# A hybrid diffusion step on one core: the second feed-forward's opening, its sums on VectorE, and matmuls ahead of the last norm

## The chip, the cores and the metric

The kernel runs on one core of a Trainium2 chip. The core has a matrix engine (TensorE, PE in the profile, with its weight loads as PEld), a vector engine (VectorE, DVE), a scalar engine (ScalarE, ACT), a general-purpose engine (GpSimd, POOL), and DMA queues, of which SyncE (SP) issues most transfers. The metric is the time of one execution on the device, in microseconds; smaller is better. Three runs of the kernel before took 2042.53, 2045.99 and 2050.24 us.

## The reference, cut to what matters

The reference is one inference step of a network of two layers over 128 context tokens and 512 latent tokens with 1024 features. Layer 0 mixes tokens with neighbourhood attention and a two-way recurrent mixer, layer 1 with differential attention. Each layer ends with a gated feed-forward of 22 x 128 = 2816 hidden features; a norm over the features closes the whole.

```python
def rmsnorm(x, g):
    xf = x.astype(jnp.float32)
    r = lax.rsqrt(jnp.mean(xf * xf, -1, keepdims=True) + NORM_EPS)
    return (xf * r).astype(x.dtype) * g

def modulate(h, shift, scale):
    return h * (1.0 + scale) + shift

def swiglu(h, w1, w3, w2):
    return (jax.nn.silu(h @ w1) * (h @ w3)) @ w2
...
    for l in range(DEPTH):
...
        xs = xs + ms[2] * ys
        xs = xs + ms[5] * swiglu(modulate(rmsnorm(xs, norm_ffn[l]), ms[3], ms[4]), ffn_w1[l], ffn_w3[l], ffn_w2[l])
```

The change concerns the feed-forward of the second layer (l = 1) and the norm behind it, for all 640 tokens (context and latent, xp and xs).

## The kernel before, in words

**Layout.** Features lie on the 128 partitions in 8 tiles (KT), tokens along the free dimension. The 640 tokens are two halves of HT = 320; one matmul has 128 x 128 weights and 320 tokens. For accuracy each factor is split in a rounded part h and a rest l (`split`: ScalarE casts to h, VectorE subtracts h to get l), and each product of two tiles is three matmuls, wh·bh, wh·bl and wl·bh (`product`: four tiles along the features, so 12 matmuls).

**The second feed-forward (`bffn`, from line 627).** Its upward projections, w1 and w3, are done by a scheme after Winograd and Strassen. Two weight tiles (a_ and a_ + 11) by two halves of the features form a 2 x 2 block matrix, and features by token halves form another; seven products do instead of eight. The activations come as B["11"], "21", "22" and the combinations t1 to t4, made by `BNorm` (`apply`: lines 580 to 611, `rest`: from 612). The weights come as "11", "12", "22" and the combinations s1 to s4, made in `prep_up`: two weight tiles r1 and r2 are loaded by SyncE (L711, L712), s1 = r2[lo] + r2[hi] (L717) and s3 = r1[lo] - r2[lo] in the place of r2[lo] (L719) are made on GpSimd, s2 and s4 on VectorE (L723, L724), and four calls of `split` (L646, L647) cast them. The raw tiles have two buffers, so the load of r2 waits until the split of an earlier tile has read its buffer. `run_up` issues the seven products for one pair and one matrix in the order 11, s1, s2, 12, s3, s4, 22. Three of these write the same PSUM tile `al` one on top of the other, and ScalarE copies `al` out in between (L757 after 11, L763 after s2, L769 after s3): the following product into `al` waits for the copy. Partials lie in the tiles `top` and `bot`, taken in turn from a pool of four (`tmp`), for w1 as for w3. `close` (L659, L660) splits the gated result.

**The opening.** The first pair (a_ = 0) is not done by the seven products but by eight plain ones for each token half, in `up_first`: four weight tiles FIRST = w1[0], w1[11], w3[0], w3[11], loaded by `plain`. The first three are loaded and split ahead of layer 1's output projection (`w_out_tail`), the fourth within the opening. Eight products on the first token half (upper features "11", lower features "21") run while the norm of the second half is computed: after the first product come the norm's sums over the features, after four more the matmul that spreads the reciprocal root over the partitions, and after three more `bn.apply(1, ps)` makes the second half's activations. After each of the upper products ScalarE copies the partial to `q` (L687). Then come four products with t1, and four with 22.

**What sets the order.** A planner orders each engine's work by the order in the program and by modelled times at which operands are there; an instruction that is ready early may be put ahead of program order, but then each engine works its list strictly in turn. While `pinned[0]` is set, TensorE's matmuls keep the program's order; that holds for the opening up to its last products. Preparations are interleaved with the products: `prep(i + 1)` advances one step after each product of item i.

**Downward projection and end.** Pairs are taken in groups (0,1), (2,3), (4,5), (6,7), (8,9,10); the downward products of a group (`run_down`) follow the first pair of the next one. The last group's are done for all but three output tiles first, then for the last three by token halves, with the final norm of a half (`Last.done`) behind each. For the second half the norm is by columns: `token_sums` (twelve entries in the profile, one column each), `rsqrt_cols` (eleven small VectorE operations) and `spread_half` (three matmuls that spread the root over the partitions), then eight VectorE multiplications and eight stores.

Of the kernel before, what the change touches and what calls it, by code (L numbers as in the profile page):

```python
# [14 lines left out]
ALU = mybir.AluOpType  # L15
# [14 lines left out]
LAST = 3  # L30
URGENT = 3000
WARM = (8, 3)
NWQ = 3
GROUPS = ((0, 1), (2, 3), (4, 5), (6, 7), (8, 9, 10))
NSQ = 1
# [55 lines left out]
def tile_backbone(ctx: ExitStack, tc: tile.TileContext, I, O, stop=99):  # L91
# [174 lines left out]

    def token_sums(ps, t, first, last):
        for j, (a, b) in enumerate(WIN):
            PE.matmul(ps[:, j:j + 1], lhsT=t[:, a:b], rhs=ones32[:, 0:1], start=first and j == 0, stop=last,
                      skip_group_check=True)  # L270

    def rsqrt_cols(ps, n, scale, eps):
        m, s, t = [SM.tile([P, n], F32, tag="r" + x, name=nm("r"), bufs=1) for x in "xyz"]
# [126 lines left out]
    class Norm:  # L400
# [18 lines left out]
        def rms(self, h, cols=False):  # L419
            assert self.n[h] == KT  # L420
            acc = self.acc[h]
            pss = one()
            if cols:
                for i, t in enumerate(acc):
                    token_sums(pss, t, i == 0, i == len(acc) - 1)
                s = rsqrt_cols(pss, 3, 1.0 / D, NORM_EPS)
                pr = one()
                spread_half(pr, s)
                return pr[:, 0:HT]
            for i, t in enumerate(acc):  # L430
                for j in range(4):
                    PE.matmul(pss[32 * j:32 * j + 32, 0:80], lhsT=ones32, rhs=t[:, 80 * j:80 * j + 80],
                              start=i == 0, stop=i == len(acc) - 1, skip_group_check=True)
            r4 = rsqrt4(pss[:, 0:80], NORM_EPS, 1.0 / D)
            pr = one()
            PE.matmul(pr[:, 0:HT], lhsT=e0, rhs=r4, start=True, stop=True)
            return pr[:, 0:HT]
# [106 lines left out]
    class BNorm(Norm):  # L544
# [8 lines left out]
        def halves(self, name, src, engines):  # L553
            a, b = unit([P, 4, HT], F32R, "bh"), unit([P, 4, HT], F32R, "bl")
            self.B[name] = a, b
            for j in range(2):
                c = slice(2 * j, 2 * j + 2)
                A.copy(a[:, c], src[:, c])
                engines[j].tensor_tensor(b[:, c], src[:, c], a[:, c], ALU.subtract)

        def done(self, h):
            if h == 0:
# [46 lines left out]
        def rest(self):  # L609
            f = self.f  # L610
            t2 = self.full("t2")

            def both(fn):
                for j in range(2):
                    fn(slice(2 * j, 2 * j + 2))

            both(lambda q: V.tensor_tensor(t2[:, q], f["22"][:, q], f["11"][:, q], ALU.subtract))
            self.halves("t2", t2, (V, G))
            yield
            both(lambda q: V.tensor_tensor(f["12"][:, q], f["22"][:, q], f["12"][:, q], ALU.subtract))  # L620
            self.halves("t3", f["12"], (V, G))
            yield
            both(lambda q: V.tensor_tensor(f["21"][:, q], f["21"][:, q], t2[:, q], ALU.subtract))
            self.halves("t4", f["21"], (V, G))
            yield

    def bffn(l, bn, xs, nx, X, w2):
# [14 lines left out]
        def flat(x):  # L642
            return x.rearrange("p k c -> p (k c)")

        def split(h, l_, src):
            A.copy(h, src)  # L646
            V.tensor_tensor(l_, src, h, ALU.subtract)  # L647

        def product(ps, w, b, first):
            (wh, wl), (bh, bl) = w, b  # L650
# [21 lines left out]
        yield  # L672

        with tc.tile_pool(name=f"wq{l}", bufs=NWQ, reuse_waits="tile") as WQ, \
                tc.tile_pool(name=f"sq{l}", bufs=NSQ, reuse_waits="tile") as SQ:
            ring[1] = WQ
            G_ = {}

# [1 line left out]
            def up_first():  # L680
                q = X.tile([P, 4, HT], F32, tag="g", name=nm("q"))
                s0 = cur["p"].tile([P, 2, 512], F32, tag="s", name=nm("be"))
                first = [one("a")[:, 0:HT], one("a")[:, 0:HT], s0[:, 0, 0:HT], s0[:, 1, 0:HT]]
                for n, b in ((0, "11"), (1, "11"), (2, "11"), (0, "21"), (1, "21"), (3, "11"), (2, "21"), (3, "21")):
                    product(first[n], Ws[n][b == "21"], B[b], b == "11")
                    if b == "11":
                        A.copy(q[:, n], first[n])  # L687
# [21 lines left out]
            def prep_up(name, a_, W):  # L709
# [4 lines left out]
                h0, l0 = two()  # L714
                split(h0, l0, r1)
                s1 = SQ.tile([P, 4, P], F32, tag="s1", name=nm("s1"))
                G.tensor_tensor(s1, r2[:, lo], r2[:, hi], ALU.add)  # L717
                yield
                G.tensor_tensor(r2[:, lo], r1[:, lo], r2[:, lo], ALU.subtract)  # L719
                hs, ls = [SQ.tile([P, 4, P], F32R, tag="s" + x, name=nm("s" + x)) for x in "hl"]  # L720
                split(hs, ls, s1)
                s24 = SQ.tile([P, KT, P], F32, tag="s2", name=nm("s2"))
# [25 lines left out]
            def run_up(name, a_, W):  # L748
# [2 lines left out]
                c = pr[a_]  # L751
                beta = c["be"][:, int(name == "w3"), 0:HT]
                al, de = one("a")[:, 0:HT], one("t")[:, 0:HT]
                top = tmp([P, 2, HT], name="top")
                bot = tmp([P, 2, HT], name="bot")
                product(al, W["11"], B["11"], True)
                A.copy(top[:, 0], al)  # L757
# [31 lines left out]
            def run_down(ms, pairs, hs, last, W):  # L789
                gs = [x for p_ in pairs for x in G_[p_]]  # L790
                gh, gl = [g for g, _ in gs], [g for _, g in gs]
                for m in ms:
                    resid(xs[m], proj([W[m]], gh, gl, psum(turn()), hs), gate, m, hs, nx if last else None)
                    yield
                if last and ms[-1] == KT - 1 and hs != (0, 1):
                    nx.done(hs[0])

# [36 lines left out]
                return iter(())  # L834

            pinned[0] = True
            uf = up_first()
            next(uf)
            ps = bn.rms1(lambda: [next(uf) for _ in range(4)])
            Ws.append(plain(*FIRST[3]))  # L840
            for _ in range(3):
                next(uf)
            bn.apply(1, ps)
            rest, nxt = bn.rest(), prep(0)
            for i, _ in enumerate(uf):
                if i == 4:
# [1259 lines left out]
```

## Time and profile before

| what | us |
|---|---|
| median of 3 runs (lowest to highest) | 2045.99 (2042.53 to 2050.24) |
| the profiled execution | 2047.56 |
| its span in the trace | 2045.8 |
| TensorE busy | 1933.3 (95%) |
| VectorE busy | 1353.2 (66%) |
| ScalarE busy | 800.1 (39%) |
| GpSimd busy | 443.8 (22%) |
| the second feed-forward in the trace | from about 1575 to the end |

The mean granted clock of TensorE in the profiled execution is 0.977 of full speed. In the views a row names the line of the code, the engine, the operation and its operands (out<-in), and where an engine stood still before an instruction, that time and what ended it stand in brackets. Line 99 is the helper through which all matmuls go. Matmuls overlap, so the distance from start to start tells the rate, not the length of one. The tile names in the rows leave out numbers: `be` is a PSUM pair, `ps` and `pp` other PSUM tiles, `s` the sums of weights, `wr` a raw weight tile, `xn`, `hb`, `bh` and `bl` stages of the norm's output.

### The profile page before, as it was taken

The page shows a single profiled execution, that of the slowest core. Times are in us where ns is not written, and L with a number is a line of the kernel's source. Part 1 is how long each engine was busy: PE and PEld are TensorE (multiplying, and loading weights), DVE is VectorE, ACT ScalarE, POOL GpSimd, SP SyncE. Part 2 cuts the span into 40 slices and gives each one's busy share as a digit, 9 for nine tenths or more (in the row PEclk, how much of TensorE's full clock was granted, in tenths as well). Part 3 has the DMA queues.
Part 4 walks back from the last instruction along what each step waited for, and adds up shares of the span by engine and source line. Part 5 has one row for each costly group of instructions (what it writes and reads, how often), then busy time and mean ns, then how long its engine had stood idle before and what let it go on. Part 6 is the DMA issues. An engine that isn't in the chain of part 4 may idle for free.

```text
span 2045.8 us, 36390 instructions
## 1 busy us (share of the span) xinstructions
PE 1933.3 (95%) x14572; PEld 1720.3 (84%) x14572; DVE 1353.2 (66%) x2695; ACT 800.1 (39%) x1585; POOL 443.8 (22%) x451
## 2 busy tenths in 40 slices
PE   6888999978999999999999999999998899999998
PEld 2777787845466899999999988989988899999997
DVE  6559657656667697733772386788787866666665
ACT  3434342322445332212222255556554544343341
POOL 1233443433130210000000034233312311111100
PEclk8999999987999999999999999999999999999998
DMA  7433233262725255432442232111012132232222
GB/s 262 146 94 104 72 100 108 82 195 87 231 68 180 97 186 175 167 112 83 157 152 68 85 105 69 51 39 58 29 42 72 56 99 73 73 93 73 83 83 75
DMA packets 106129, 214.21 MB, mean 105 GB/s; under 512 B 33384, under 2 KB 43624, under 8 KB 102632
## 3 DMA queue, kind: packets, MB, share of 16 engines
q1 hardware_dynamic: 99080, 172.31, 27.1%
q0 software_dynamic: 6880, 39.59, 5.4%
q8 instruction: 114, 1.87, 0.4%
q14 instruction: 55, 0.45, 0.1%
HBM read 190.36 MB, written 23.44 MB: 105 GB/s over the span
## 4 chain that ended last, share of the span: by engine, by line
PE 63%; DVE 11%; DMA 4%; ACT 3%; issue 2%; POOL 1%; SPq 0%; ACTq 0%; DVEq 0%; POOLq 0%
PE ps L99 33%; PE pp L99 16%; PE c L99 2%; PE be L99 2%; PE sd L99 2%; DMA wr<-in_w 2%; PE psc L99 1%; PE y L99 1%; PE pj L99 1%; PE sna L99 1%; PE pa L99 1%; DVE mt L1186 1%; DVE wl L647 1%; PE po L99 1%; DVE mi L1187 1%
## 5 line engine op out<-in xcount | busy, mean ns | idle before, releaser
L344 ACT CAST wh<-wr 128x1024 fp32r<-128x1024 f32 (+3 forms) x174 | 143.1, 824 | 426.4 <-issue 189.0
L347 DVE TENSOR_TENSOR wl<-wr,wh 128x1024 fp32r<-128x1024 f32 (+2 forms) x124 | 130.4, 1054 | 130.5 <-ACT wh L344 129.6
L99 PE MATMUL ps<-hh,wh 128*128 128x320 f32 x592 | 185.7, 314 | 0.0
L99 PE MATMUL ps<-hl,wh 128*128 128x320 f32 x592 | 185.4, 313 | 0.2
L99 PE MATMUL ps<-hh,wl 128*128 128x320 f32 x592 | 185.2, 313 | 0.0
L99 PE MATMUL pj<-hh,wh 128*128 128x320 f32 x416 | 135.9, 328 | 7.6 <-ACT wh L344 5.0
L99 PE MATMUL ps<-bh,wh 128*128 128x320 f32 x432 | 134.9, 312 | 7.8 <-ACT top L757 6.4
L99 PE MATMUL pj<-hl,wh 128*128 128x320 f32 x416 | 137.5, 331 | 0.3 <-POOL hl L308 0.2
L99 PE MATMUL pj<-hh,wl 128*128 128x320 f32 x416 | 135.8, 327 | 1.5 <-POOL wl L347 1.5
L99 PE MATMUL ps<-bh,wl 128*128 128x320 f32 x432 | 134.1, 310 | 0.0
L99 PE MATMUL ps<-bl,wh 128*128 128x320 f32 x432 | 134.0, 310 | 0.0
L216 DVE SCALAR_TENSOR_TENSOR av<-wa,cs,av 128x512 f32<-128x512 f32 x182 | 123.9, 746 | 0.0
L347 POOL TENSOR_TENSOR wl<-wr,wh 128x512 fp32r<-128x512 f32 (+1 forms) x50 | 72.2, 1448 | 204.9 <-ACT wh L344 187.7
L99 PE MATMUL pp<-hh,wh 128*128 128x320 f32 x368 | 115.5, 314 | 0.0
L99 PE MATMUL pp<-hh,wl 128*128 128x320 f32 x368 | 114.0, 310 | 0.0
L99 PE MATMUL pp<-hl,wh 128*128 128x320 f32 x368 | 113.8, 310 | 0.0
L99 PEld LDWEIGHTS ps<-hh,wh 128*128 128x128 f32 x592 | 111.6, 189 | 2.2 <-ACT hh L465 0.8
L99 PEld LDWEIGHTS ps<-hl,wh 128*128 128x128 f32 x592 | 111.6, 188 | 2.1 <-issue 0.8
L99 PEld LDWEIGHTS ps<-hh,wl 128*128 128x128 f32 x592 | 111.6, 189 | 1.7 <-issue 1.5
L646 ACT CAST wh<-wr 128x1024 fp32r<-128x1024 f32 (+1 forms) x71 | 72.0, 1014 | 101.8 <-PE ps L99 61.0
L647 DVE TENSOR_TENSOR wl<-wr,wh 128x1024 fp32r<-128x1024 f32 (+1 forms) x71 | 88.8, 1251 | 16.0 <-ACT wh L646 15.8
L383 DVE SCALAR_TENSOR_TENSOR x<-ps,ada,x 128x192 f32<-128x192 f32 (+2 forms) x156 | 63.5, 433 | 50.2 <-PE ps L99 50.0
(409 smaller groups left out, 5625.9 us busy)
## 6 DMA issues: line engine op xcount, KB each, us to landing
wr<-in_w SPq DMA_DIRECT2D x88, 512.0 KB, 3.6
wa<-in_w_ada POOLq DMA_DIRECT2D x26, 1024.0 KB, 5.2
wa<-in_w_ada SPq DMA_DIRECT2D x88, 256.0 KB, 5.0
wr<-in_w_qk SPq DMA_DIRECT2D x16, 512.0 KB, 3.5
wr<-in_w2s SPq DMA_DIRECT2D x16, 512.0 KB, 3.6
wr<-in_w SPq DMA_DIRECT2D x19, 384.0 KB, 3.2
wr<-in_w_in_u SPq DMA_DIRECT2D x28, 256.0 KB, 2.9
wr<-in_w_in_qk SPq DMA_DIRECT2D x24, 256.0 KB, 2.9
```

Of the source, the lines that this page charges most:

```text
L99: i = nc.tensor.matmul(*a, **k)
L216: V.scalar_tensor_tensor(out=acc[s], in0=w[:, j], scalar=c, in1=acc[s], op0=ALU.mult, op1=ALU.add)
L344: A.copy(wh[:, 0:n], raw[:, 0:n])
L347: eng.tensor_tensor(wl[:, 0:n], raw[:, 0:n], wh[:, 0:n], ALU.subtract)
L383: V.scalar_tensor_tensor(out=xk[:, a:b], in0=pp[h][:, a - HT * h:b - HT * h], scalar=gate[:, m, s:s + 1], in1=xk[:, a:b], op0=ALU.mult, op ...
L646: A.copy(h, src)
L647: V.tensor_tensor(l_, src, h, ALU.subtract)
L1186: V.tensor_tensor(t3, bc(mi[:, rows, jj], 2, w), bc(mi[:, jj, cols], 1, jj), ALU.mult)
L1187: V.tensor_tensor(mi[:, rows, cols], mi[:, rows, cols], t3, ALU.add)
```

## The change

1. In `up_first` the four upper products ("11") come first, then the four lower ones ("21"). The fourth weight tile is loaded and split ahead of the opening, not within it.
2. The first `split` behind the opening's norm is ordered, on ScalarE and on VectorE, behind the last cast and the last subtraction of the norm (`gate_`, `lastA`, `lastV`). These are orders within an engine, without a semaphore.
3. The subtractions for the second half of t2, t3 and t4, and the weight sums s1 and s3, move from GpSimd to VectorE.
4. `top` of w3 gets a pool with one buffer of its own (`TP_`, 2,560 bytes a partition).
5. Between the column sums of the last norm and its spread, twelve matmuls on a constant operand (`cur["full"]`, the first gated tile of the last group) write the PSUM tile that the spread then overwrites; they are ordered behind the sums.

```diff
+NWARM = 12
...
     def token_sums(ps, t, first, last):
         for j, (a, b) in enumerate(WIN):
-            PE.matmul(ps[:, j:j + 1], lhsT=t[:, a:b], rhs=ones32[:, 0:1], start=first and j == 0, stop=last,
-                      skip_group_check=True)
+            i = PE.matmul(ps[:, j:j + 1], lhsT=t[:, a:b], rhs=ones32[:, 0:1], start=first and j == 0, stop=last,
+                          skip_group_check=True)
+        return i
...
-                    token_sums(pss, t, i == 0, i == len(acc) - 1)
+                    at_ = token_sums(pss, t, i == 0, i == len(acc) - 1)
                 s = rsqrt_cols(pss, 3, 1.0 / D, NORM_EPS)
                 pr = one()
+                w = cur["full"]
+                for _ in range(NWARM):
+                    i = PE.matmul(pr[:, 0:HT], lhsT=w[:, 0:P], rhs=w[:, 0:HT], start=True, stop=True)
+                    tc.add_manual_dep(i.ins, at_.ins.name, NOSYNC, reason="in between")
+                    at_ = i
                 spread_half(pr, s)
...
-                A.copy(a[:, c], src[:, c])
-                engines[j].tensor_tensor(b[:, c], src[:, c], a[:, c], ALU.subtract)
+                self.lastA = A.copy(a[:, c], src[:, c])
+                self.lastV = engines[j].tensor_tensor(b[:, c], src[:, c], a[:, c], ALU.subtract)
...
-            self.halves("t2", t2, (V, G))
+            self.halves("t2", t2, (V, V))
...
-            self.halves("t3", f["12"], (V, G))
+            self.halves("t3", f["12"], (V, V))
...
-            self.halves("t4", f["21"], (V, G))
+            self.halves("t4", f["21"], (V, V))
...
+        gate_ = [None]
+
         def split(h, l_, src):
-            A.copy(h, src)
-            V.tensor_tensor(l_, src, h, ALU.subtract)
+            i = A.copy(h, src)
+            j = V.tensor_tensor(l_, src, h, ALU.subtract)
+            if gate_[0] is not None:
+                for x, y in zip((i, j), gate_[0]):
+                    tc.add_manual_dep(x.ins, y.ins.name, NOSYNC, reason="the norm goes first")
+                gate_[0] = None
...
+                tc.tile_pool(name=f"tp{l}", bufs=1, reuse_waits="tile") as TP_:
...
-                for n, b in ((0, "11"), (1, "11"), (2, "11"), (0, "21"), (1, "21"), (3, "11"), (2, "21"), (3, "21")):
+                for n, b in ((0, "11"), (1, "11"), (2, "11"), (3, "11"), (0, "21"), (1, "21"), (2, "21"), (3, "21")):
...
-                G.tensor_tensor(s1, r2[:, lo], r2[:, hi], ALU.add)
+                V.tensor_tensor(s1, r2[:, lo], r2[:, hi], ALU.add)
...
-                G.tensor_tensor(r2[:, lo], r1[:, lo], r2[:, lo], ALU.subtract)
+                V.tensor_tensor(r2[:, lo], r1[:, lo], r2[:, lo], ALU.subtract)
...
-                top = tmp([P, 2, HT], name="top")
+                top = tmp([P, 2, HT], name="top", pool=TP_ if name == "w3" else None)
...
+                cur["full"] = gh[0]
...
             pinned[0] = True
+            Ws.append(plain(*FIRST[3]))
             uf = up_first()
             next(uf)
             ps = bn.rms1(lambda: [next(uf) for _ in range(4)])
-            Ws.append(plain(*FIRST[3]))
             for _ in range(3):
                 next(uf)
             bn.apply(1, ps)
+            gate_[0] = (bn.lastA, bn.lastV)
```

More of the change, by code (lines that the diff above doesn't have):

```diff
@@ L674, in bffn @@
         with tc.tile_pool(name=f"wq{l}", bufs=NWQ, reuse_waits="tile") as WQ, \
-                tc.tile_pool(name=f"sq{l}", bufs=NSQ, reuse_waits="tile") as SQ:
+                tc.tile_pool(name=f"sq{l}", bufs=NSQ, reuse_waits="tile") as SQ, \
+                tc.tile_pool(name=f"tp{l}", bufs=1, reuse_waits="tile") as TP_:
             ring[1] = WQ
```

## The prediction

> **What bounds the kernel now.** I read the page first, for the share of each engine.
>
> ```profile
> span 2045.8 us, 36390 instructions
> PE 1933.3 (95%) x14572; PEld 1720.3 (84%) x14572; DVE 1353.2 (66%) x2695; ACT 800.1 (39%) x1585; POOL 443.8 (22%) x451
> ```
>
> TensorE is busy 95% of the span and the change takes no product away. So it can only win time in which TensorE waits, or runs slowly, inside the stage that the diff touches: from 1575 us, where the second feed-forward opens, to the end. The waits of TensorE there come next, first from 1575 to 1640 us, then from 1640 to 2015 us (columns: total, times, longest).
>
> ```profile
> PE ps L99 <- ACT top L757: 3.0, 2, 2.2
> PE be L99 <- ACT q L687: 2.6, 1, 2.6
> PE ps L99 <- ACT top L763: 1.4, 1, 1.4
> ```
> ```profile
> PE ps L99 <- ACT top L757: 3.4, 4, 1.2
> ```
>
> There are 7.0 us of waits in 65 us of opening, and only 3.4 us in the 375 us behind it. The chain that ended last shows that waiting costs more than itself (start, length, number of matmuls):
>
> ```profile
> 1596.86 8.78 PE be L99 x48
> 1637.23 3.20 PE ps L99 x12
> ...
> 1672.46 3.52 PE pp L99 x24
> ```
>
> The last row is the full rate: 24 matmuls in 3.52 us, 0.147 us each. The 12 matmuls at 1637.23 should take 1.76 us and take 3.20, a loss of 1.44; the 48 at 1596.86 should take 7.04 and take 8.78, a loss of 1.74. Both rows begin where a long wait ends. The stretches of 10 us say why (PE, PEld, DVE, ACT and POOL busy, then the granted clock):
>
> ```profile
> 1590.00:1600.00 10.00, 7.39 (x40) 6.97 (x39) 8.40 (x14) 5.67 (x12) 1.42 (x1) 0.84 0.18 55
> 1610.00:1620.00 10.00, 9.72 (x67) 9.45 (x65) 9.79 (x12) 5.42 (x9) 7.86 (x4) 1.00 0.19 54
> 1630.00:1640.00 10.00, 7.82 (x47) 7.55 (x46) 6.24 (x8) 4.70 (x8) 3.11 (x2) 0.88 0.23 68
> ```
>
> The granted clock falls in exactly the two stretches with the waits of 2.6 and 2.2 us; in the stretch with 0.8 it stays at 1.00. So 10.2 us can be had in the opening (7.0 + 1.44 + 1.74) and 3.4 behind it: 13.6 us, 0.7% of the time. A difference below about 0.5% (10.2 us) cannot be told from no change by a measurement of this kernel.
>
> **Part A, the opening products in two runs.** Before, the fourth upper product came after two lower ones, and the next lower product waited for its copy.
>
> ```profile
> 1591.78 0.70 PE L99 MATMUL ps<-r,cst 128*128 128x320 f32 x2
> 1593.94 0.31 PE L99 MATMUL be<-bh,wl 128*128 128x320 f32 x1
> ```
> ```profile
> 1583.57 1.21 DVE L647 TENSOR_TENSOR wl<-wr,wh 128x1024 fp32r<-128x1024 f32 x1
> ...
> 1594.29 1.23 DVE L647 TENSOR_TENSOR wl<-s,wh 128x1024 fp32r<-128x1024 f32 x1 [1.11 <-ACT wh L646]
> 1595.43 2.29 DVE L591 TENSOR_TENSOR xn<-x,ps 128x320 f32<-128x320 f32 x5
> 1600.45 0.82 DVE L559 TENSOR_TENSOR bl<-hb,bh 128x640 fp32r<-128x640 f32 x1
> ```
> ```profile
> 1595.95 0.55 ACT L596 ACTIVATE hb<-xn,ada,gsc 128x192 f32<-128x192 f32 x1 [1.69 <-DVE xn L591]
> 1596.40 0.40 ACT L687 COPY q<-be 128x320 f32<-128x320 f32 x1
> ```
>
> The product was finished at 1594.1, yet its copy ran at 1596.40: ScalarE takes its work in order, and ahead of the copy stood the norm's first activation, which waited for VectorE's xn, and xn stood behind a weight split at 1594.29. With four upper products first, the copy precedes the spread of the norm (1591.78). The fourth product now needs its weights earlier; their split is the work moved up, and VectorE already ends one such split at 1584.8, ahead of the product's new place (1588), so I cost it at nothing; without that cover it would be its 1.2 us. The wait (2.6) and the slow matmuls (1.74) go. Eight products without them end at 1594.1 + 2 x 1.76 = 1597.6.
>
> What is late next is the operand t1. From the first xn to the end of its first lower half (1595.43 to 1600.45 + 0.82) are 5.84 us, less 0.3 for the copy that is no longer in between. If xn starts as the spread ends, at 1592.5, t1 is there at 1598.0, a new wait of 0.4. If the weight sums, which the new order does not hold back (it holds only the first split behind the norm), take VectorE for one or two more 0.7 us operations, it is 1.2. I take 0.8: A gains 2.6 + 1.74 - 0.8 = 3.5. Bounds: 0.8 if xn still starts at 1595.43 (t1 at 1601.3, where the eight products now end at 1596.86 + 3.52 + 1.74 = 1602.1), 4.3 with no wait.
>
> **Part B, sums and splits on VectorE, in the opening.** Groups from 1580 to 2030 us (count, busy, mean ns, idle before), then one line of the view of tile s (minimum, median, maximum):
>
> ```profile
> L719 POOL TENSOR_TENSOR wr<-wr,wr 128x512 f32<-128x512 f32 x20 | 35.1, 1753 | 1.6
> L717 POOL TENSOR_TENSOR s<-wr 128x512 f32<-128x512 f32 x20 | 27.0, 1351 | 288.2 <-DMA wr<-in_w 236.0 <-ACT wh L646 45.2 <-PE be L99 6.9
> L559 POOL TENSOR_TENSOR bl<-hb,bh 128x640 fp32r<-128x640 f32 x3 | 8.1, 2716 | 17.4 <-ACT bh L558 17.4
> ```
> ```profile
> L724 DVE TENSOR_TENSOR s<-wr,s 128x512 f32<-128x512 f32 x20 | 22.2, 1111 | 0.3
> ```
> ```profile
> L724 DVE TENSOR_TENSOR s<-wr,s x20: 674/680/1674, 1592.5 to 1957.8; 128x512 f32<-128x512 f32 x20
> ```
>
> Forty GpSimd operations of 1.35 and 1.75 us become VectorE operations of the same shape as L724, 0.68 us at its median; three of 2.72 become 0.82 (the L559 row above). VectorE gets 40 x 0.68 + 3 x 0.82 = 29.7 us. It gives some back: L724 averages 1.11 against its median of 0.68, because it runs beside L719; 20 x 0.43 = 8.6 us. Net 21 us on 1353, so VectorE goes from 66 to 67%. The SBUF page of the Trainium skill ("SBUF — State Buffer", section "Who interferes with whom") has a VectorE operation with two inputs in SBUF lock out a GpSimd operation that reads SBUF, and the reverse; the doubled L724 agrees with it.
>
> Each set of sums hangs on a transfer, and the later waits of the opening on the sums:
>
> ```profile
> 1626.07 4.50 DMA wr<-in_w
> 1630.74 1.28 POOL s L717
> ...
> 1633.13 1.32 DVE s L724
> ```
> ```profile
> 1636.75 0.43 ACT L757 COPY top<-ps 128x320 f32<-128x320 f32 x1
> ```
>
> From landing (1630.6) to the end of L724 (1634.45) are 3.9 us, to the copy that TensorE waited for 6.1. Four VectorE operations in a row, both sums, L723 and L724, are 4 x 0.68 = 2.7, so the copy comes 1.2 us sooner behind the landing. TensorE, however, arrives 3.5 us sooner by A, while the transfer only comes as much sooner as the split before it, which frees its buffer. That split waits for the opening's own weights to be used up, so it too moves with A. I therefore count the 1.2 us of shortening on the wait of 2.2, which leaves about 1.0, too short for the clock to fall (+1.44), and half of the two waits of 0.8 and 1.4 (+1.1): B gains 1.2 + 1.44 + 1.1 = 3.7. Bounds: a loss of 2, if A's head start only lengthens these waits and the clock still falls; a gain of 5.9 if all go.
>
> **Part C, the same and the buffer for the upper partials, behind the opening.** Once in each group of pairs the chain goes through the sums, and TensorE waits 0.86 us on average (3.4 in four waits above), 1.2 at most:
>
> ```profile
> 1716.33 3.42 DMA wr<-in_w
> 1719.89 1.30 POOL s L717
> 1721.22 0.70 DVE s L723
> 1721.94 1.67 DVE s L724
> ```
>
> From landing (1719.8) to the end of L724 (1723.6) are 3.8 us. The same four make 2.7: 1.1 us sooner, more than the average wait. The copy top (L757) that TensorE waits for also no longer needs a tile that a later multiplication frees, as the w3 half has its own. I take 3.0 of 3.4. Bounds 0 and 3.4; a loss is a rival below.
>
> **Part D, twelve constant matmuls ahead of the last spread.**
>
> ```profile
> 2032.49 1.70 PE L99 MATMUL ps<-ones,sq 128*128 128x1 f32 x12 [0.41 <-ACT sq L412]
> 2036.41 1.84 PE L99 MATMUL ps<-cst,r 128*128 128x128 f32 x6 [2.22 <-DVE r L279]
> ```
> ```profile
> 2032.00:2034.00 2.00, 1.58 (x13) 1.51 (x12) 0.44 (x2) 0.91 (x2) 0.00 (x0) 0.91 0.43 150
> 2034.00:2036.00 2.00, 0.19 (x1) 0.10 (x1) 1.46 (x9) 0.00 (x0) 0.00 (x0) 0.50 0.00 0
> ```
>
> Twelve at 0.147 are 1.8 us and fit into the wait of 2.2; then the spread would run at the full clock, in 0.9 instead of 1.84. But the clock fell before the wait, under the one-column sums. At half rate twelve take 12 x 0.27 = 3.2 us, 1.0 more than the wait. Bounds: gain 0.9, loss 1.0; I take 0, as a late spread at full clock ends where it does now. By the page "TensorE: Matmul & The Clock Gate" of the Trainium skill, section "What's actually happening", full rate needs about 3.4 us of sustained work; so the twelve would run slow, the spread too, and the sum be 1.0 smaller. The two drops after waits of 2.6 and 2.2 us say that less than its whole idle window is enough to fall.
>
> **Sum.** 3.5 + 3.7 + 3.0 + 0 = 10.2 us. The profiled execution took 2047.56 us (its span 2045.8 and 1.8 around it), so 2037.4 for one like it. It lies 1.6 above the median of the runs, 2045.99; from that, 2035.8, which I round to 2036.
>
> **Rivals.**
> 1. VectorE becomes the bound of the opening. For it: 9.79 of 10 us busy from 1610 to 1620, and the splits of t2 to t4 now come there too. Against: the operations stretched beside GpSimd shrink. Then A's 3.5 us come back as waits in B, one slow clock stretch goes and C stays: 1.7 + 3.0 = 4.7, 2041.3. [...]
> 2. The weight sums still come before the norm, as the split at 1594.29 did. The idle time of VectorE before the spread speaks for it, its sums being free to slip in; against, they are shorter now and can be over by 1592.5. A shrinks to 0.8: 7.5 in all, 2038.5.
> 3. Slower: VectorE waits for transfers in GpSimd's place. L717 let GpSimd idle 288 us, 236 of it for a DMA; VectorE works in order, so the evictions (L766, L772) and the splits queued behind a sum would wait, ScalarE's casts behind these, and then TensorE's copies, which have the 1.76 us of one product as cover. From 0.36 us of TensorE per preparation (20 of them) A and B are eaten up, from 0.87 it is slower by 0.5%; at 1.0 us it is 20 - 7.2 = 12.8 longer, 2058.8. Against: VectorE already waits for GpSimd's sum there, so it is parked behind the same transfer today.
> 4. The order of work barely moves and the waits stay: 2046.
> 5. The twelve matmuls run at half rate and so does the spread behind them: 1.0 lost, 2036.8. The fall of the clock ahead of the wait speaks for it; against, twelve matmuls at half rate are 3.2 us of dense work, about as long as the slow stretch at 1596.86 lasted. The clock page named in part D speaks for it as well.
>
> **How the numbers follow.** Forecast 0.58, rivals 0.15, 0.08, 0.07, 0.04 and 0.08. The forecast's own range, from the bounds of A to D without the worst of each, is 2031 to 2041. To leave out no more than 2 in 10 I take 2030 to 2046: all 13.6 us and the tail's gain with the spread of the runs, up to no change; rival 3 stays out. Faster by over 0.5% means below 2035.8: 0.36 of the forecast's 0.58, as what is to be had (13.6) reaches further beyond the sum than the losses counted in it, 0.03 of rival 5 and 0.02 of rivals 1 and 2, together 0.41. Slower: 0.06, nearly all rival 3. The rest, 0.53, is within 0.5%.
>
> **What would show it.** A: no wait of TensorE for the copy q, xn starting within a microsecond of the spread, a wait for t1 below 1.5 us. B: clock 1.00 in the stretches that answer to 1590 and 1630 us. C: no wait for top behind 1640, L724 near 0.68 on average. D: the spread's start and length. It is wrong if VectorE's first sum stands idle on a DMA while TensorE waits, or if waits for t2 to t4 appear.

## The result, and the profile after

The changed kernel takes 2030.11 us (median of six runs, 2028.01 to 2035.71), the kernel before 2045.12 (six runs of the same comparison, 2041.68 to 2050.24). The ratio is 0.9935 with a 95% interval of 0.9920 to 0.9949. It is faster by 0.65%, or 15.0 us by the medians. The forecast was 2036, within a range of 2030 to 2046.

The profiled execution took 2028.79 us, of which 2027.0 are its span. The line of the engines on its page:

```profile
PE 1926.1 (95%) x14584; PEld 1716.4 (85%) x14584; DVE 1356.6 (67%) x2738; ACT 801.0 (40%) x1585; POOL 374.0 (18%) x408
```

GpSimd lost 70 us of work, and VectorE, which took it over, is busy only 3.4 us longer (1353.2 before). The waits of TensorE from 1560 us to the end (total, times, longest):

```profile
PE ps L100 <- DVE xn L598: 0.7, 1, 0.7
PE ps L100 <- ACT sq L414: 0.6, 2, 0.4
PE be L100 <- ACT q L701: 0.5, 1, 0.5
PE ps L100 <- DVE acc L416: 0.2, 1, 0.2
PE be L100 <- DVE bl L566: 0.2, 1, 0.2
```

All waits for the copy top are gone, and so is the one of 2.2 us for the inverse roots at the very end, whose place the constant matmuls fill. In windows (length, then PE, PEld, DVE, ACT, POOL busy, granted clock, DMA share, GB/s) the opening looks like this:

```profile
1580.00:1600.00 20.00, 19.29 (x127) 18.34 (x126) 17.48 (x34) 14.37 (x29) 0.00 (x0) 1.00 0.06 24
1600.00:1620.00 20.00, 20.00 (x137) 19.81 (x137) 19.45 (x29) 13.39 (x22) 0.00 (x0) 1.00 0.23 66
1620.00:1640.00 20.00, 20.00 (x138) 20.00 (x137) 17.32 (x25) 12.27 (x20) 0.00 (x0) 1.00 0.29 96
```

The granted clock, 0.84 and 0.88 in two stretches of the opening before, is 1.00 throughout, and TensorE stands still for 0.7 us of 60, although VectorE is busy 19.45 of 20 us in the middle.

To compare kernels whose stages begin at different times, I cut the span by rows that all of them have. These are the cuts of after, from the timeline: the root of the norm on VectorE, the first matmul of the first and of the last group's downward products, the last twelve column sums, the first step of the inverse root, and the first row of the output; the twelve constant matmuls and the spread stand between them.

```profile
1578.47 0.23 DVE L254 TENSOR_SCALAR rm<-ps 128x80 f32<-128x80 f32 x1
...
1656.33 0.46 PE L100 MATMUL pp<-g,wh 128*128 128x320 f32 x2
...
1966.09 0.46 PE L100 MATMUL pp<-g,wh 128*128 128x320 f32 x2
...
2012.05 2.08 PE L100 MATMUL ps<-ones,sq 128*128 128x1 f32 x12 [0.42 <-ACT sq L414]
2014.00 3.55 PE L100 MATMUL ps<-g 128*128 128x320 f32 x12
2014.17 0.16 DVE L276 TENSOR_SCALAR r<-ps 128x3 f32<-128x3 f32 x1 [2.17 <-PE ps L100]
...
2017.34 1.67 PE L100 MATMUL ps<-cst,r 128*128 128x128 f32 x6
2019.05 3.76 DVE L1946 SCALAR_TENSOR_TENSOR y<-x,small,ps 128x320 f32<-128x320 f32 x8 [2.75 <-PE ps L100]
```

The opening is 1656.33 - 1578.47 = 77.86 us, the groups 1966.09 - 1656.33 = 309.76, the tail 2019.05 - 2012.05 = 7.00 and its last part, from root to output, 2019.05 - 2014.17 = 4.88. The same for all runs (times of a run's comparison are in the sections below):

| run | begins at | opening | groups | tail | root to output |
|---|---|---|---|---|---|
| before | 1584.78 | 87.52 | 314.23 | 5.80 | 4.06 |
| after | 1578.47 | 77.86 | 309.76 | 7.00 | 4.88 |
| a1_order | 1581.04 | 86.52 | 314.09 | 5.60 | 4.06 |
| a2_vector | 1581.28 | 79.07 | 309.76 | 5.60 | 4.06 |
| a3_top | 1580.25 | 87.04 | 317.65 | 6.34 | 4.06 |
| a4_nowarm | 1582.44 | 77.82 | 309.76 | 5.60 | 4.06 |
| b1_nogate | 1580.74 | 78.30 | 309.76 | 4.84 | 3.30 |
| b2_notop | 1585.50 | 77.83 | 309.76 | 5.74 | 4.20 |
| b3_sumspool | 1582.42 | 83.98 | 314.15 | 7.05 | 4.88 |
| b4_tpool | 1578.53 | 81.23 | 309.76 | 7.34 | 4.87 |
| c1_bystander | 1583.43 | 82.25 | 318.05 | 5.75 | 4.21 |
| c2_triple | 1582.98 | 77.99 | 310.65 | 6.79 | 4.88 |
| c3_s3pool | 1582.51 | 81.09 | 309.76 | 6.81 | 4.88 |
| c4_warm5 | 1589.58 | 77.84 | 309.76 | 6.32 | 4.06 |

So the 18.8 us between the two profiled spans are 9.66 in the opening, 4.47 in the groups, -1.20 in the tail, -0.44 behind it, and 6.31 that lie ahead of anything the change touches. Eight kernels agree on 309.76 us for the groups: that is TensorE without a wait.

The 6.31 us can be seen in one pair of rows, first of before, then of after:

```profile
475.00:500.00 25.00, 25.00 (x206) 16.02 (x206) 10.31 (x37) 3.66 (x12) 6.67 (x8) 0.75 0.13 27
```
```profile
475.00:500.00 25.00, 24.99 (x248) 15.10 (x247) 12.85 (x42) 5.12 (x15) 8.68 (x11) 1.00 0.29 76
```

Up to the opening both kernels run the same 11591 matmuls. In these 25 us the clock was 0.75 in one and 1.00 in the other, and 206 and 248 matmuls ran. It is no gain of the change: the start of the opening lies anywhere from 1578.5 to 1589.6 us in the table. The gain of the touched stages is 9.66 + 4.47 - 1.20 - 0.44 = 12.5 us; the 15.0 of the medians holds a share of this scatter.

### The profile page after: what moved, and what is told of

It is laid out like the page before. It is cut to its first block, busy times and chain, and to the rows that moved or that the text cites. A ratio compares the mean times of both kernels' runs of the same rounds, so it can differ in the third digit from the quotient of the medians.

```text
span 2027.0 us, 36329 instructions
## 1 busy us (share of the span) xinstructions
PE 1926.1 (95%) x14584; PEld 1716.4 (85%) x14584; DVE 1356.6 (67%) x2738; ACT 801.0 (40%) x1585; POOL 374.0 (18%) x408
## 4 chain that ended last, share of the span: by engine, by line
PE 68%; DVE 7%; DMA 3%; ACT 3%; issue 1%; POOL 1%; SPq 0%; DVEq 0%; ACTq 0%; POOLq 0%
PE ps L100 38%; PE pp L100 16%; PE be L100 2%; PE c L100 2%; PE sd L100 2%; PE pa L100 1%; PE psc L100 1%; PE sna L100 1%; PE y L100 1%; PE pj L100 1%; DVE mi L1203 1%; PE po L100 1%; PE pt L107 1%; DMA wr<-in_w_out 1%; DVE wl L349 1%
## 5 line engine op out<-in xcount | busy, mean ns | idle before, releaser
L656 DVE TENSOR_TENSOR wl<-wr,wh 128x1024 fp32r<-128x1024 f32 (+1 forms) x71 | 83.8, 1180 | 18.7 <-ACT wh L655 17.1
```

The lines of the kernel that those rows point to most:

```text
L656: j = V.tensor_tensor(l_, src, h, ALU.subtract)
```

## The experiments

My theory once the result was known: GpSimd's two sums per weight tile were what TensorE waited for, and the order of the opening gave less than predicted. The rivals: order first, sums second (as predicted); and the top buffer as the cause in the groups. The b and c kernels ran once each, beside single runs of before of 2050.22 and 2042.36 us, so they are read by the stretches of their traces and not by their times.

**a1_order: before, with the order alone.** The gate that puts the norm ahead of the next split is not in it.

```diff
-                for n, b in ((0, "11"), (1, "11"), (2, "11"), (0, "21"), (1, "21"), (3, "11"), (2, "21"), (3, "21")):
+                for n, b in ((0, "11"), (1, "11"), (2, "11"), (3, "11"), (0, "21"), (1, "21"), (2, "21"), (3, "21")):
...
             pinned[0] = True
+            Ws.append(plain(*FIRST[3]))
             uf = up_first()
...
-            Ws.append(plain(*FIRST[3]))
```

> The kernel before with the new order of the opening alone: four upper products, then four lower ones, and the fourth weight tile loaded and split ahead. Three stretches are compared in each trace: the opening, from VectorE's first operation of the second half's root (rm) to the first matmul of the first downward products (87.7 us before, 78.0 after the change); the groups, from there to the first matmul of the last group's downward products (314.2 and 309.8); the tail, from the last column sums to the first multiplication with the norm (5.8 and 7.0). Theory 1 (the prediction's part A stands by itself): the wait for the copy q and the slow clock behind it go, the opening takes 84 us (3.5 less), groups and tail stay. Rival (what is won is given back at the later waits of the opening): 87 to 88 us.

One execution took 2042.45 us, beside a median of 2044.06 of before. The opening became only 1.00 us shorter, between the two expectations. Waits of TensorE that are new or changed, then the norm's spread, the weight split on VectorE and the norm's first xn in the timeline:

```profile
PE be L99 <- ACT bh L558: 1.5, 1, 1.5
...
PE be L99 <- DVE bl L559: 0.6, 1, 0.6
PE be L99 <- ACT q L687: 0.5, 1, 0.5
```
```profile
1588.82 0.70 PE L99 MATMUL ps<-r,cst 128*128 128x320 f32 x2
...
1590.53 1.23 DVE L647 TENSOR_TENSOR wl<-s,wh 128x1024 fp32r<-128x1024 f32 x1 [1.12 <-ACT wh L646]
...
1591.67 2.07 DVE L591 TENSOR_TENSOR xn<-x,ps 128x320 f32<-128x320 f32 x5
```

The wait for q fell from 2.6 to 0.5, but xn still stood behind the split: it came 2.85 us after the spread began and 10.63 us behind the root's first step, where it was 10.65 before. TensorE waited 1.5 and 0.6 us for t1 instead. The clock from 1590 to 1600 us was 0.86 all the same.

**a2_vector: before, with the sums and the splits of t2 to t4 on VectorE alone.**

```diff
-            self.halves("t2", t2, (V, G))
+            self.halves("t2", t2, (V, V))
...
-                G.tensor_tensor(s1, r2[:, lo], r2[:, hi], ALU.add)
+                V.tensor_tensor(s1, r2[:, lo], r2[:, hi], ALU.add)
                 yield
-                G.tensor_tensor(r2[:, lo], r1[:, lo], r2[:, lo], ALU.subtract)
+                V.tensor_tensor(r2[:, lo], r1[:, lo], r2[:, lo], ALU.subtract)
```

(t3 and t4 as t2.)

> The kernel before with the sums s1 and s3 and the splits of t2 to t4 on VectorE, and nothing else. Theory 1 (the sums on GpSimd held ScalarE's copies up): the four waits behind the opening go, groups 310 to 311 us instead of 314.2; of the opening the wait of 2.2 us and its slow clock go, 84 to 86; the wait of 2.6 us for q stays. Theory 2 (the copies were held up by the place of the tile top, not by the sums): groups stay at 313 to 314 us, opening 87.

It took 2030.58 us: 8.45 of the 9.66 us of the opening and all 4.47 of the groups. The opening of 79.07 us is far below the 84 to 86 expected, and the wait for q did not stay at 2.6:

```profile
PE be L99 <- ACT q L687: 0.8, 1, 0.8
```

With the old order and without the gate it is 0.8 us. VectorE is through with its sums sooner and starts xn 7.75 us behind the root's first step instead of 10.65, with the weight split behind it. So the wait hung on VectorE coming late to xn, and the new order is not the only thing that takes it away.

**a3_top: before, with the own buffer for the upper partials alone.**

```diff
-                top = tmp([P, 2, HT], name="top")
+                top = tmp([P, 2, HT], name="top", pool=TP_ if name == "w3" else None)
```

> The kernel before with a buffer of its own for top of w3, and nothing else. Theory 1 (the sums): the waits for the copy top stay, groups 313 to 314 us. Theory 2 (the place of top): ScalarE copies top as soon as the product is there, the four waits go, groups 310 us, and of the opening the waits for this copy (0.8 and 2.2 us) go, 84 us or less.

It took 2046.49 us, and the groups became 3.4 us longer, which neither theory expected; the wait for top rose from 6.4 to 9.9 us:

```profile
PE ps L99 <- ACT top L758: 9.9, 7, 2.7
```

**b2_notop: after, without that buffer.** The diff is the one above, reversed.

> The changed kernel with top of w3 taken from the common pool again. Theory (with the sums on VectorE the place of top does not matter, as these alone gave 309.8 for the groups without it): opening 78, groups 309.8. Rival (the buffer is needed once the order of the opening is changed): a wait for the copy top comes back, opening 79 to 81 or groups 310.5 and more.

2033.69 us in one execution; opening and groups are those of after to 0.03 us, and its span is longer ahead of the opening alone (it begins at 1585.5). The buffer is worth nothing beside the rest. Why it does harm by itself I did not find out.

**b3_sumspool: after, with both sums back on GpSimd.** It undoes the second half of a2's diff.

> The changed kernel with the weight sums s1 and s3 on GpSimd again, the splits of t2 to t4 still on VectorE. Theory (the sums are what counts, as they stand between each transfer and ScalarE's casts): groups 313 to 318 us with waits for the copy top, opening 82 to 87. Rival (the splits of t2 to t4, each 2.7 us on GpSimd, are what counts in the opening): opening 80 or less, groups alone go up.

2043.09 us; opening +6.12, groups +4.39, as the theory expected. Rows of VectorE's operations from 1570 to 2012 us, and TensorE's waits:

```profile
L738 DVE TENSOR_TENSOR s<-wr,s 128x512 f32<-128x512 f32 x20 | 22.5, 1126 | 0.3
...
L737 DVE TENSOR_TENSOR s<-s,wr 128x512 f32<-128x512 f32 x20 | 14.9, 743 | 41.8 <-POOL s L731 41.8
```
```profile
PE ps L100 <- ACT top L777: 4.0, 2, 2.6
PE ps L100 <- ACT top L771: 3.3, 4, 1.0
```

With the sums on GpSimd the four waits for top in the groups are back (3.3 us, 3.4 before). The opening has two of them with 4.0 us, where it had three with 4.4 before. VectorE idles 41.8 us for GpSimd (39.7 before). The same view of after (L731 is the first sum, now on VectorE), and then of before, where these rows answer to it:

```profile
L656 DVE TENSOR_TENSOR wl<-wr,wh 128x1024 fp32r<-128x1024 f32 x57 | 69.6, 1222 | 17.0 <-ACT wh L655 15.7 <-PE ps L100 1.3
...
L731 DVE TENSOR_TENSOR s<-wr 128x512 f32<-128x512 f32 x20 | 13.8, 688 | 10.5 <-DMA wr<-in_w 10.5
L656 DVE TENSOR_TENSOR sl<-s,sh 128x512 fp32r<-128x512 f32 x20 | 13.7, 687 | 14.0 <-ACT sh L655 13.9
L738 DVE TENSOR_TENSOR s<-wr,s 128x512 f32<-128x512 f32 x20 | 13.7, 685 | 0.1
```
```profile
L647 DVE TENSOR_TENSOR wl<-wr,wh 128x1024 fp32r<-128x1024 f32 x57 | 74.7, 1310 | 14.4 <-ACT wh L646 14.4
...
L647 DVE TENSOR_TENSOR sl<-s,sh 128x512 fp32r<-128x512 f32 x20 | 16.4, 820 | 11.3 <-ACT sh L646 11.3
```

These subtractions of VectorE are shorter with GpSimd idle, not only the one that stood right beside its sum.

b3_sumspool is also the one run that has order and gate together while GpSimd makes the sums. Its spread and xn:

```profile
1590.18 0.70 PE L100 MATMUL ps<-r,cst 128*128 128x320 f32 x2
...
1590.92 2.08 DVE L598 TENSOR_TENSOR xn<-x,ps 128x320 f32<-128x320 f32 x5 [0.47 <-PE ps L100]
```

There xn starts 0.74 us behind the spread, TensorE waits 0.5 us for q and 0.2 for t1, and the clock from 1590 to 1600 us is 1.00.

**b4_tpool: after, with the second halves of t2 to t4 split on GpSimd.**

> The changed kernel with half of the splits of t2 to t4 on GpSimd again, the sums on VectorE. Theory (the sums count): groups 309.8, opening 78 to 80. Rival (these splits set the opening): opening 82 or more, with waits of TensorE for bl.

2031.87 us; the opening is 3.37 us longer, between the two expectations, and the groups are unchanged. TensorE waits 1.1 us once for VectorE's additions into q (L715), not for an operand bl, and 1.1 us once for top. Why these come late I did not trace.

**b1_nogate: after, without the gate.**

```diff
-            gate_[0] = (bn.lastA, bn.lastV)
```

> The changed kernel without the order that puts the first weight split behind the norm. Known so far: with sums and splits on VectorE alone the opening took 79.1 us and the groups 309.8, against 78.0 and 309.8 of the whole change. Theory (the gate is worth a part of the last 1.2 us): opening 78.5 to 79.5, groups 309.8. If the gate does nothing: 77.8. If without it the norm comes late by a split and a cast as in the kernel before: 80 or more.

2028.55 us in one execution. The opening is 0.44 us longer, between no effect and the 78.5 us expected at least: with the sums on VectorE the norm nearly goes first by itself.

**Contention or length of the chain?** GpSimd's sums could cost TensorE in two ways. They lie between a tile's landing and its halves, and they are slower than VectorE's (1.35 us against 0.69). Or they slow the work that VectorE does beside them. Two kernels were to take these apart. c1_bystander starts from b2_notop and gives GpSimd as much work per tile, which nobody waits for; c2_triple lengthens the chain by two VectorE operations and leaves GpSimd idle.

```diff
                 V.tensor_tensor(s1, r2[:, lo], r2[:, hi], ALU.add)
+                dm = SQ.tile([P, 4, P], F32, tag="dm", name=nm("dm"))
+                G.tensor_tensor(dm, s1, s1, ALU.add)
                 yield
                 V.tensor_tensor(r2[:, lo], r1[:, lo], r2[:, lo], ALU.subtract)
...
+                G.tensor_tensor(dm, dm, s1, ALU.subtract)
```

> The changed kernel without the top buffer (which moved neither stretch), plus two operations of 128x512 per weight tile on GpSimd whose result nobody uses: the sum of s1 with itself and that minus s1. Nothing of the computation is left out. GpSimd so has as much to do per tile as before the change, but nothing that TensorE needs waits for it. Theory 1 (contention: VectorE's subtractions of the weights are stretched while GpSimd works beside them): the mean of the weight subtraction goes from 0.69 us back to above 0.95 us, the stretch of the weight groups from 309.8 to 312-314 us, the opening from 77.8 to 79.5 us or more; the time is 2036 us or more. Theory 2 (chain: what counted is that GpSimd's two sums lay between a tile's landing and its halves): the subtractions may be stretched, but the groups stay at 309.8 to 310.5 us and the opening at 78 to 79 us; the time is 2028 to 2034 us.

```diff
                 V.tensor_tensor(s1, r2[:, lo], r2[:, hi], ALU.add)
+                V.tensor_tensor(s1, r2[:, lo], r2[:, hi], ALU.add)
+                V.tensor_tensor(s1, r2[:, lo], r2[:, hi], ALU.add)
```

> The changed kernel with the sum s1 of each weight tile issued three times in a row on VectorE (the same values each time), so that each tile's halves stand about 1.2 us later behind its landing, without any work on GpSimd. Theory 1 (contention alone): VectorE has slack, the groups stay at 309.8 to 310.5 us and the opening at 77.8 to 78.8 us; the time is about 2030 us. Theory 2 (chain from landing to halves): it is as long again as with GpSimd's sum of 1.35 to 1.75 us in place of 0.6 us, so the groups go to 312-314 us and the opening to 80-83 us; the time is 2035 to 2042 us.

c1_bystander took 2045.63 us (before, on the same chip, 2042.36): opening +4.42, groups +8.29 against b2_notop. Its rows of VectorE's operations (L740 is L737 of after, L741 is L738), and its waits for top:

```profile
L740 DVE TENSOR_TENSOR s<-s,wr 128x512 f32<-128x512 f32 x20 | 25.7, 1283 | 0.0
...
L741 DVE TENSOR_TENSOR s<-wr,s 128x512 f32<-128x512 f32 x20 | 19.3, 963 | 0.1
```
```profile
PE ps L100 <- ACT top L774: 6.5, 5, 1.7
```

VectorE never waits for GpSimd there, and in the chain its own operations are longer, these two by their means 1.28 and 0.96 us instead of 0.69. That brings 6.5 us of waits for this copy back, adds 2.4 us of waits for bot, and makes the groups longer than before and than the 312 to 314 us expected. c2_triple took 2033.99 us: opening +0.13 and groups +0.89 against after, with one wait for top:

```profile
PE ps L100 <- ACT top L773: 0.6, 1, 0.6
```

So contention alone is enough for a loss of 12.7 us, against the 14.1 that the change gained in the two stretches. It is somewhat stronger than before, though: GpSimd's two operations keep it about as busy (64.8 us, 62.1 before), but VectorE's two take 2.25 us together, where they took 1.91. The groups of c2_triple came 0.15 us above the 310.5 that contention alone allowed. Its 2034 us missed the "about 2030"; it began 4.5 us later than after.

c2_triple does not show that the chain counts little, as its order of work is another one. The planner knows of the two added operations and puts ScalarE's cast of the sums (wh<-s) behind the copy top for which TensorE waits in the groups; c1_bystander has it ahead, as before and after have. ScalarE in c1_bystander, then in c2_triple:

```profile
1718.92 1.06 ACT L655 CAST wh<-s 128x1024 fp32r<-128x1024 f32 x1 [2.85 <-DVE s L741]
...
1723.77 0.42 ACT L774 COPY top<-ps 128x320 f32<-128x320 f32 x1
```
```profile
1715.95 0.41 ACT L773 COPY top<-ps 128x320 f32<-128x320 f32 x1
...
1718.24 1.05 ACT L655 CAST wh<-s 128x1024 fp32r<-128x1024 f32 x1
```

Where the order is that of before, this copy comes 4.9 to 5.3 us behind the end of the last sum, and TensorE's waits in the groups follow the length of the chain ahead of it, from the start of the first sum to the end of the last. The chain takes 3.02 us in after and 3.13 in c3_s3pool (below), and there is no wait; 3.73 in before and b3_sumspool, and the four waits are 0.86 and 0.83 us on average; 4.57 in c1_bystander, and they are 1.57. (In a3_top it is 3.73 as well, and one of the four waits is 2.7 us: there the sum began later, as its transfer landed later.) One chain of after, and one of c1_bystander:

```profile
1703.14 0.69 DVE L731 TENSOR_TENSOR s<-wr 128x512 f32<-128x512 f32 x1 [1.42 <-DMA wr<-in_w]
...
1705.48 0.68 DVE L738 TENSOR_TENSOR s<-wr,s 128x512 f32<-128x512 f32 x1
```
```profile
1714.27 0.69 DVE L731 TENSOR_TENSOR s<-wr 128x512 f32<-128x512 f32 x1 [3.01 <-DMA wr<-in_w]
...
1717.45 1.39 DVE L741 TENSOR_TENSOR s<-wr,s 128x512 f32<-128x512 f32 x1
```

So contention and the chain are not rivals in the groups: contention costs TensorE time by making the chain longer. Both had a part before: in the chain that part C of the prediction shows, the first sum took 1.30 us on GpSimd, and L724 1.67 beside the second one, where after has 0.69 and 0.68. For the opening no run takes the two apart.

**c3_s3pool: after, with only the second sum (s3) on GpSimd.**

```diff
-                V.tensor_tensor(r2[:, lo], r1[:, lo], r2[:, lo], ALU.subtract)
+                G.tensor_tensor(r2[:, lo], r1[:, lo], r2[:, lo], ALU.subtract)
```

> The changed kernel with only the second sum of each tile (r1 minus r2) on GpSimd, the first one on VectorE. With both on GpSimd the opening was 84.0 us and the groups 314.2 us, with both on VectorE 77.8 and 309.8. If the first sum is the one that counts (the casts of s1 stand right behind it on ScalarE): opening 78-79.5 us, groups 309.8-310.5 us, about 2030 us. If each sum counts alike: opening about 81 us, groups about 312 us, about 2036 us. If the second one counts (the sum of four, s2, hangs on it): opening 82-84 us, groups 313-314 us, about 2042 us.

2036.82 us; opening +3.23, in three new waits of 0.8 to 0.9 us, as if each sum counted alike, but groups +0.00. None of the three expectations fits both. The subtraction beside it (L738) is stretched to 1105 ns as it was before (1111). The chain is still only 0.11 us longer than in after, since the second sum no longer takes VectorE's time within it, and in the groups that costs nothing; with both sums on GpSimd it is 0.71 longer, and TensorE waits.

**The constant matmuls: a4_nowarm (none) and c4_warm5 (five), both from after.**

```diff
-NWARM = 12
+NWARM = 0
```

> The changed kernel without the twelve constant matmuls. If they cost time as the trace after the change shows (they run at half rate and hold the spread up): the tail is 5.8 us as before the change, 1.2 shorter than with them, opening and groups as after the change (78.0 and 309.8), the whole 1 to 1.5 us faster than the changed kernel's 2030, which rounds of 0.1% hardly tell. If the tail of 7.0 us was an accident of where the clock's fall lay, it is 5.8 to 7 here too and the whole does not change.

```diff
-NWARM = 12
+NWARM = 5
```

> The changed kernel with five constant matmuls ahead of the last spread in place of twelve. At half the clock twelve took 3.55 us where the wait for the inverse roots is 2.2 us; five would take 1.4 to 1.5 us and are done before the roots at either clock. Theory of the twelve being too long: the tail (from the first of the last column sums to the first row of the output) is 5.6 to 5.8 us with a spread of 1.5 to 1.7 us, or 4.8 us with a spread of 1.07 us if the clock happens to stay; not 6.5 to 7.3 us as in four of the five runs with twelve of which the clock fell earlier. If the tail is 6.5 us or more, it wasn't their number. The time is 2028 to 2032 us either way.

a4_nowarm took 2030.42 us (four executions, 2027.87 to 2032.63), a ratio to before of 0.9926 (interval 0.9904 to 0.9947), against 0.9935 of after: not to be told apart. Its tail of 5.60 us is as short as the first expectation had it, in a run in which the clock fell late. c4_warm5 took 2038.56, outside its 2028 to 2032, as it began latest of all (1589.58); its tail of 6.32 us lies between the two theories, because the clock fell early in its column sums (2.22 us where a4_nowarm shows 1.50). The part behind them is not touched by that; the spread of c4_warm5:

```profile
2027.57 1.84 PE L100 MATMUL ps<-cst,r 128*128 128x128 f32 x6 [0.68 <-DVE r L281]
```

The spread of b1_nogate, where the clock stayed at 1.00:

```profile
2018.47 1.07 PE L100 MATMUL ps<-cst,r 128*128 128x128 f32 x6 [0.36 <-DVE r L281]
```

From the root to the output every run without constant matmuls takes 4.06 us, and so does the one with five. With twelve, five of eight runs take 4.87 or 4.88, two 4.20 and 4.21, and one 3.30. It depends on whether the clock falls ahead of them (in after they take 3.55 us, and the spread starts 3.17 us behind the root's first step, where it is 2.18 in c4_warm5), among them, or not at all.

## Why the prediction was right, and where its steps were not

The forecast, faster by 10 us with a range down to 2030, held; its range only just, with 2030.11. The gain of the touched stages was 12.5 us where the sum said 10.2; 2045.12 less 12.5 would be 2032.6, so the last 2.5 us are scatter of the untouched part. That the sum came this near is in part luck: the opening gave 2.5 and the groups 1.5 us more than forecast, and the tail and what lies behind it took back 1.6.

**What bounds the kernel: right, but 1.1 us too small in the groups.** The gain lies in the waits and clock falls that were counted. The wait of 0.8 us lies for the most part behind the stretch from 1610 to 1620 beside which the prediction put it, but from 1620 to 1630, with the rest of it and the wait of 1.4, the clock was 1.00 too. A wait costs more than its row. Before, in the timeline of one in the groups:

```profile
1728.47 0.31 PE L99 MATMUL ps<-bh,sl 128*128 128x320 f32 x1
1729.42 0.42 PE L99 MATMUL ps<-bh,wh 128*128 128x320 f32 x1 [0.64 <-ACT top L757]
1729.67 0.31 PE L99 MATMUL ps<-bl,wh 128*128 128x320 f32 x1
```

From the first start to the third are 1.20 us instead of 2 x 0.147: 0.91 lost for a wait of 0.64. The wait is counted from the end of a matmul, 0.31 us after its start, where the next would have started after 0.147, and the start behind the first matmul after the wait comes after 0.25. Reckoned like this the four waits of the groups cost 4.48 us, and 4.47 were gained; in b3_sumspool they cost 4.39, which is just what its groups are longer.

**A, order and gate, 3.5 us: the mechanism held, the size is not shown for these two alone.** The order alone gave 1.00, near the bound of 0.8 named for an xn that starts where it did, and there it stood behind a weight split, as the prediction had read it. With the gate (b3_sumspool) xn came right behind the spread, and the opening was 3.54 us shorter than before; but the splits of t2 to t4 and the top buffer are in that run too. On top of a2_vector, order, gate and top buffer gave only 1.21. The step that failed is to add A and B as separate gains: the sums on VectorE bring xn forward by themselves, so that A is worth less where B is. "No wait for q" was wrong by 0.5 us: the fourth product writes the tile be while its other half is being copied, and TensorE waits for that copy, which is the 0.5 for q that after still shows. xn within a microsecond of the spread (0.74) and a wait for t1 below 1.5 us (0.2) came true:

```profile
1586.24 0.70 PE L100 MATMUL ps<-r,cst 128*128 128x320 f32 x2
...
1586.98 2.08 DVE L598 TENSOR_TENSOR xn<-x,ps 128x320 f32<-128x320 f32 x5 [1.58 <-PE ps L100]
```

**B, sums and splits in the opening, 3.7 us: undersized.** On top of order and gate the sums alone gave 6.12 (after against b3_sumspool), above the bound of 5.9, and the splits 3.37 (b4_tpool); without order and gate both together gave 8.45. The term that was too small is the share of the three waits for top, of which the prediction left about half: in after all of them are gone. The step that fell short is the cost on VectorE: it gave back not 8.6 us by L724 alone, but about 26.7, as it took over 27.6 us of sums and about 2.5 of splits and is busy 3.4 longer. Besides L724, the weight splits fell from 1310 to 1222 ns (57 of them) and the splits of the sums from 820 to 687 (20). That a VectorE which is this much shorter reaches xn, the splits and the partials early is how I read the opening; how much of the gain is this and how much the shorter chain is not shown there. The Trainium skill, on the page "SBUF — State Buffer", section "Who interferes with whom", says that a VectorE operation with two inputs in SBUF contends with a GpSimd instruction that reads SBUF; the 0.69 to 1.28 us of c1_bystander agree. The prediction had that rule beside it and used it for one line only.

**C, the groups, 3.0 of 3.4: right, with 4.47 measured**, by the sum above. The chain became 0.7 us shorter (3.73 to 3.02), not 1.1, as another addition of VectorE (L780) now stands within it, and that was enough for all four waits. The top buffer has no part in it (b2_notop). L724, near 0.68 as predicted, is at 685 ns.

**D, the constant matmuls, 0: 0.82 lost between root and output in the profiled execution**, inside the bounds of +0.9 and -1.0. The step "a late spread at full clock ends where it does now" failed by its condition: the clock was 0.50 from 2013 to 2019 us, and the spread, 1.0 us later, took 1.67 us, hardly less than 1.84. The other 0.38 of the tail are the column sums, during which the clock fell earlier. The 0.44 behind the tail I did not trace.

**The rivals.** VectorE as the bound of the opening (1): 19.45 of 20 us busy and TensorE without a wait; it fell. Sums ahead of the norm (2): in after they do come first (1582.17 to 1585.39), but are over before the spread, for which VectorE then waits 1.58 us, as the prediction had against it; without the gate they are over in time as well. a1_order shows the lateness as long as GpSimd has the sums. VectorE parked behind transfers (3): it idles 10.5 us at its first sum, and no wait of TensorE answers to that. Order without effect (4) fell. Twelve matmuls at half rate (5) came in five of eight runs, at 0.82 instead of 1.0 us. It could not be told in the forecast's time because it decides 0.04% of it.

## What to carry to other kernels

That GpSimd is idle does not make work on it free: ask what VectorE does in the same microseconds, and add up the stretch of all its operations there, not of one line. Vector operations moved back to VectorE can cost VectorE almost nothing, here 3.4 us for 30. Where a planner orders the work, an added operation can change the order (c2_triple): compare the order of the engines before the times are read. Compare kernels stage by stage between rows that both have: in this one the part that nobody touched moved by 11 us from run to run, nearly as much as the change gained.

## What was not expected of the hardware

The clock's falls differ from run to run, by more than the filler in the tail is worth. The same 11591 matmuls ahead of the opening were done 11.1 us apart (at 1578.47 in after, at 1589.58 in c4_warm5); the two rows of 475 to 500 us show a clock of 0.75 in before and 1.00 in after. The Trainium skill, on the page "TensorE: Matmul & The Clock Gate", section "What's actually happening", says that the activity window is free-running, so that the number of slow matmuls varies from run to run. The runs agree that it varies, though none shows the window itself; here it is 0.5% of the time, and it has to be kept out of a verdict on a change of that size. That the twelve column sums at the end keep TensorE's row busy did not keep its clock up: in after they took 2.08 us, in c4_warm5 2.22, and 1.50 where the fall came later.
